# Preamble reordered on VectorE and ScalarE, the keys' norm table in one chain, and five unread products on TensorE between its first steps

## The chip, the cores and the metric

The kernel runs on one core of a Trainium2 chip. The metric is device time in microseconds (us) of one execution, lower is better. TensorE (PE, with its weight loads PEld), VectorE (DVE), ScalarE (ACT), GpSimd (POOL) and SyncE (SP) each take their own instructions in the order in which they were put down, and wait for each other through semaphores. Transfers are issued by SP, POOL and ACT.

## The reference

A decoder trunk of two layers over 512 tokens of width 2048. Each layer normalises its input, projects it once to 7696 columns, feeds three groups of heads, and projects the result back into the residual stream:

```python
def _layer(x, norm_g, w_in, conv_w, conv_b, sb_qn_g, sb_kn_g, gla_w_up, gla_b_up, gla_on_g, w_out):
    h = _rmsnorm(x, norm_g)                      # mean of squares over 2048, times a gain
    proj = h @ w_in                              # (512, 2048) @ (2048, 7696), split into 13 parts
    y_conv = _short_conv(cv_h, cv_b, cv_c, conv_w, conv_b) * silu(cv_g)
    q = _rmsnorm(sb_q.reshape(b, s, 8, 128), sb_qn_g)
    k = _rmsnorm(sb_k.reshape(b, s, 8, 128), sb_kn_g)
    y_sb = _stick_breaking(q, k, v) * silu(sb_g)
    g = log_sigmoid(gl_lr @ gla_w_up + gla_b_up) / 16
    y_gla = _rmsnorm(_gla(gl_q, gl_k, gl_v, g), gla_on_g) * silu(gl_g)
    return x + concatenate([y_conv, y_sb, y_gla]) @ w_out
```

## The kernel before

**Blocks and passes.** The 512 tokens are four blocks of 128 (`t` 0 to 3). The weights go through in blocks of 256 columns, listed in `specs`; the first of layer 0 are "gla v 0" (block 0), "gla v 1" with 16 narrow columns (block 1, 272 wide), "gla q" (block 2), "gla k" (block 3), "gla gate 0" (block 4). Every float32 operand is split into a float16 high half and a float16 low half, and each product is made of three: high by high, high by low, low by high. Weight blocks 0 and 1 are projected by token (`project_by_token`, line 857): 48 products for each token block, 16 of them high activations by high weights, 16 low activations by high weights, 16 high activations by low weights. Blocks 2 and 3 are projected by column (`project_cols`, lines 702 to 704) in two banks. Some later blocks, "gla gate 0" first, use fewer products on sums of token blocks (`xsums`, line 735; ACT's part is line 743).

**The preamble of layer 0.** For each token block: `xsquare(t)` sums squares on ACT, `xnorm` makes the scale (ACT and four small steps on DVE), `xgain(t, h)` multiplies half a block by scale and gain on DVE (h is the half of the 2048 columns), `xhigh(t, h)` transposes eight 128x128 pieces on TensorE (line 591) and copies them from PSUM as the float16 high half (line 593, tile `x`), and `xlow(t, h)` makes the low half: for block 0 on TensorE (line 603, adding the negative high half) and ACT (line 604), for the others by a subtraction on DVE (line 600). The gain row itself is spread over the partitions by twelve products (`spread`, line 244).

**The weights.** `fetch(i)` loads block i in two halves into one of two stage buffers (tile `st`). `wpeak0` and `wmax` square it on ACT (line 383), `wscale` turns the sums into a power of two (tile `ws`), `whi` or `whi0` writes the high half (tile `wh`, on ACT lines 445 and 454, on DVE line 447), `wlo` the low half (tile `wl`, line 461, DVE). For block 0 the sums over partitions are three small products (line 409). Blocks 0 to 2 are fetched by SP, later ones by POOL, each as soon as the last reader of its stage buffer is done.

**What sets the order.** On DVE and ACT the preamble is inside `tc.manual_schedule`: those calls stand in the written order. All else, and TensorE, SP and POOL throughout, is placed by a scheduler that follows priorities and dependencies; `order(a, b)` adds an edge without a wait. So the scheduler may put the token sums, the constants (`layer_consts`, lines 292 to 312) and the split of the results (`split_v`, lines 948 and 949) between preamble steps. Products by token and by column share one pool of three PSUM banks (`psp`), given out in turn: a bank is free when its readers are done, and for block 1 these are `split_v` and the copy of the 16 narrow columns (tile `lr`, line 975). The transposes use two double banks (`psz`).

**The norm table.** `layer_consts` transposes the small parameters (line 294) into `par` and for each layer on its own forms the product of the two norm gains, its maximum over partitions (POOL, line 183), a power of two (tiles `kpc`, `zun`), a diagonal matrix, and a product with ones (line 310), copied into `kg` (line 311).

Of the kernel before, what the change touches and what calls it, by code (L numbers as in the profile page):

```python
# [10 lines left out]
AF = mybir.ActivationFunctionType  # L11
# [6 lines left out]
P = 128  # L18
# [25 lines left out]
def hybrid_trunk(ctx, tc, x, norm_g, w_in, conv_w, conv_b, sb_qn_g, sb_kn_g,  # L44
# [193 lines left out]
    gps_ = [bank2(), bank2()]  # L238

    def spread(h):  # L240
        for a in range(2):
            r = 2 * h + a
            for i in range(3):
                T.matmul(gps_[h][:, a, :], identb[:4, r:r + 1].to_broadcast([4, P]), g3[:, i, :], start=i == 0,
                         stop=i == 2)
# [21 lines left out]
    for h in range(2):  # L267
        spread(h)
# [23 lines left out]
    def layer_consts():  # L292
        pps = bank(psm, "m")
        T.transpose(pps[:, :NP], prow, ident[:NP, :NP])
        V.tensor_copy(par, pps[:, :NP])
        for l in range(depth):
            V.tensor_reduce(onmax[:, l:l + 1], pcol("on", l), AX.X, ALU.max, apply_absolute_value=True)
            V.tensor_scalar(onmax[:, l:l + 1], onmax[:, l:l + 1], float(P) ** 0.5, None, ALU.mult)

            gq = sm(2, "cm")  # L300
            V.scalar_tensor_tensor(gq[:, 0:1], pcol("qn", l), float(P) ** -0.5, pcol("kn", l), ALU.mult, ALU.mult)
            V.tensor_scalar(gq[:, 1:2], allmax(gq[:, 0:1], 1, "k"), 2.0 ** -20, None, ALU.max)
            pow2(zun[:, l:l + 1], gq[:, 1:2], -20.0, "k")
            V.tensor_scalar(nzun[:, l:l + 1], zun[:, l:l + 1], -1.0, None, ALU.mult)
            V.reciprocal(gq[:, 1:2], zun[:, l:l + 1])

            dg = wk([P, P], "e")
            V.tensor_scalar(gq[:, 0:1], gq[:, 0:1], gq[:, 1:2], 2.0 ** -21, ALU.mult, ALU.mult)
            V.tensor_scalar(dg, ident, gq[:, 0:1], None, ALU.mult)
            T.matmul(pps[:, (l + 1) * P:(l + 2) * P], ones.to_broadcast([P, P]), dg, start=True, stop=True)  # L310
            V.tensor_copy(kg[:, l, :], pps[:, (l + 1) * P:(l + 2) * P])
            V.tensor_scalar(nbu[:, l, :], par[:, base["bu"] + 2 * l:base["bu"] + 2 * l + 2], -1.0, None, ALU.mult)
# [79 lines left out]
    def wscale(i):  # L392
# [10 lines left out]
        else:  # L403
# [4 lines left out]
            for j, (a, b) in enumerate(((ones, pk[:, 0:1]), (ones, pk[:, 1:2]), (pk[:, 2:3], pk[:, 2:3]))):  # L408
                T.matmul(ps, a.to_broadcast([P, P]), b, start=j == 0, stop=j == 2)
# [173 lines left out]
    xps = {}  # L583

    def xhigh(t, h, dst):
# [3 lines left out]
        for i in range(HK):  # L589
            k = h * HK + i  # L590
            T.matmul(ps[:, i, :], xv[:, k * P:(k + 1) * P], ident, start=i % 4 == 0, stop=True, is_transpose=True,
                     skip_group_check=True)
        S.activation(dst[0][:, t, h * HK:(h + 1) * HK, :], ps, AF.Copy)
# [49 lines left out]
    xsquare(1)  # L643
    wscale(0)
    whi0(0, 0, S)
    whi0(0, 1, V)
    xhigh(0, 1, mix)
# [6 lines left out]
    xlow(0, 1, mix, True)  # L654
    wlo(0, 0)
    wlo(0, 1)
    xhigh(1, 0, mix)
    xhigh(1, 1, mix)
    xsquare(2)
    xlow(1, 0, mix, False)  # L660
    xlow(1, 1, mix, False)
    xnorm(0, 2)
    xgain(2, 0)
    xgain(2, 1)
    xsquare(3)
    xnorm(0, 3)
    xhigh(2, 0, mix)
    xhigh(2, 1, mix)
    wmax(1, 0)
    xgain(3, 0)  # L670
    xgain(3, 1)
    xlow(2, 0, mix, False)
    xlow(2, 1, mix, False)
    wmax(1, 1)
    wscale(1)
    xhigh(3, 0, mix)
    xhigh(3, 1, mix)
    whi(1, 0)
    xlow(3, 0, mix, False)
    xlow(3, 1, mix, False)  # L680
    wlo(1, 0)
# [4 lines left out]
    for l in range(depth):  # L686
# [162 lines left out]
        def project_by_token(ah, al, n):  # L849
# [3 lines left out]
            for t in range(NT):  # L853
# [7 lines left out]
                ps.append(o)  # L861
                yield t, o, u
# [91 lines left out]
        if l == 0:  # L954
            layer_consts()
# [62 lines left out]
        for tag in ("qT", "kT"):  # L1018
# [520 lines left out]
```

## Time and profile before

| | before |
|---|---|
| median of 3 runs | 1634.72 us (1633.69 to 1635.13) |
| profiled execution | 1635.55 us |
| its span | 1633.8 us |
| PE, PEld busy | 1615.5 us (99%), 1356.8 us (83%) |
| DVE busy | 1446.2 us (89%) |
| ACT busy | 1196.5 us (73%) |
| POOL busy | 269.4 us (16%) |
| DMA moved | 235.98 MB, mean 144 GB/s |

The span runs from the first to the last instruction; the execution's time has some start and end around it. A matmul counts as busy from its start to the modelled end of its pipeline, so a busy TensorE may still be slow. The time from one start to the next tells its speed.

### The profile page before, as it was taken

How to read it: one execution, taken by the hardware profiler on the slowest of the kernel's cores; microseconds unless marked ns; L12 is line 12 of the kernel's file. 1: busy time of each engine (PE TensorE's matmuls, PEld its weight loads, DVE VectorE, ACT ScalarE, POOL GpSimd, SP SyncE). 2: the span in 40 equal slices, each digit the busy share in tenths (PEclk: the TensorE clock that was granted, in tenths of full speed). 3: DMA queues.
4: the chain of work that ended last, by engine and by line, in shares of the span. 5: the costliest groups of instructions: out<-in, count | busy, mean ns of one | idle time of the engine just before them, and what ended most of it. 6: DMA issues, size and time to landing. Idle time of an engine off the chain costs nothing.

```text
span 1633.8 us, 42252 instructions
## 1 busy us (share of the span) xinstructions
PE 1615.5 (99%) x18202; PEld 1356.8 (83%) x18202; DVE 1446.2 (89%) x2417; ACT 1196.5 (73%) x1771; POOL 269.4 (16%) x306
## 2 busy tenths in 40 slices
PE   8999999999999999999999999999999999999998
PEld 5757768989899968799996668689898989668998
DVE  7989989989898979898699899898998889898896
ACT  7668887977777776756775697788786868676573
POOL 0122021111212122011102111212121211220110
PEclk9999999999999999999999999999999999999999
DMA  7244435477767686644743544545777786773441
GB/s 262 81 103 145 89 119 111 106 164 144 169 150 169 150 169 186 177 148 147 244 94 107 127 117 103 144 89 137 155 158 160 153 165 150 161 229 130 156 157 54
DMA packets 193643, 235.98 MB, mean 144 GB/s; under 512 B 90242, under 2 KB 153036, under 8 KB 192944
## 3 DMA queue, kind: packets, MB, share of 16 engines
q0 software_dynamic: 79904, 181.42, 42.2%
q1 hardware_dynamic: 104544, 42.42, 13.4%
q10 hardware_dynamic: 9008, 9.45, 1.8%
q8 instruction: 142, 2.33, 0.6%
q14 instruction: 45, 0.37, 0.1%
HBM read 179.65 MB, written 14.68 MB: 119 GB/s over the span
## 4 chain that ended last, share of the span: by engine, by line
PE 68%; DVE 16%; ACT 7%; DMA 5%; issue 3%; POOL 1%; SPq 0%; DVEq 0%; ACTq 0%; POOLq 0%
PE psp L798 22%; PE psp L795 13%; PE psp L857 6%; PE psp L714 4%; PE psp L713 4%; PE psp L715 4%; PE psp L703 3%; PE psp L702 3%; DVE wl L509 3%; PE psp L704 3%; DMA st<-in_w_in_dram 3%; ACT wh L508 1%; PE psm L1345 1%; ACT junk L383 1%; PE psz L1305 1%
## 5 line engine op out<-in xcount | busy, mean ns | idle before, releaser
L508 ACT ACTIVATE wh<-st,ws 128x1024 f16<-128x1024 f32 x270 | 300.7, 1144 | 170.5 <-DVE st L528 89.8
L509 DVE SCALAR_TENSOR_TENSOR wl<-st,ws,wh 128x1024 f16<-128x1024 f32 x270 | 340.3, 1283 | 28.4 <-ACT wh L508 28.3
L383 ACT ACTIVATE junk<-st 128x2048 uint8<-128x2048 f32 x150 | 285.4, 1903 | 14.7 <-DMA st<-in_w_out_dram 6.9
L795 PE MATMUL psp<-s,wh 128*128 128x256 f16 x1280 | 217.7, 273 | 1.0 <-DVE g L811 0.9
L795 PEld LDWEIGHTS <-wh 128*128 128x128 f16 x1920 | 187.4, 98 | 23.3 <-issue 1.4
L798 PE MATMUL psp<-wh,s 128*128 128x128 f16 x2048 | 177.1, 219 | 0.5 <-issue 0.4
L795 PE MATMUL psp<-s,wl 128*128 128x256 f16 x640 | 174.3, 273 | 0.9 <-DVE wl L509 0.9
L713 PE MATMUL psp<-wh,m 128*128 128x256 f16 x640 | 174.5, 273 | 0.0
L715 PE MATMUL psp<-wh,m 128*128 128x256 f16 x640 | 174.5, 273 | 0.0
L714 PE MATMUL psp<-wl,m 128*128 128x256 f16 x640 | 174.5, 273 | 0.0
L798 PEld LDWEIGHTS <-s 128*128 128x128 f16 x3072 | 173.0, 98 | 0.8 <-issue 0.7
L798 PE MATMUL psp<-wl,s 128*128 128x128 f16 x1024 | 173.3, 219 | 0.0
L461 DVE SCALAR_TENSOR_TENSOR wl<-st,ws,wh 128x2048 f16<-128x2048 f32 x62 | 145.0, 2349 | 15.0 <-ACT wh L454 13.8
L362 POOL DMA_DIRECT2D st<-in_w_in_dram x114 | 109.7, 1030 | 246.4 <-DVE w7l L509 118.3
L798 PEld LDWEIGHTS <-m 128*128 128x128 f16 x2448 | 139.1, 98 | 2.1 <-issue 1.6
L454 ACT ACTIVATE wh<-st,ws 128x2048 f16<-128x2048 f32 x60 | 118.6, 1999 | 16.0 <-DVE ws L415 7.9
L399 POOL PARTITION_ALL_REDUCE wgm<-wm x75 | 48.1, 641 | 461.2 <-ACT junk L383 446.0
L386 POOL DMA_DIRECT2D st<-st x36 | 57.2, 1590 | 350.8 <-ACT junk L383 331.5
L795 PEld LDWEIGHTS <-wl 128*128 128x128 f16 x960 | 93.9, 98 | 14.4 <-issue 2.1
L798 PE MATMUL psp<-wh,m 128*128 128x128 f16 x1088 | 97.2, 219 | 0.4 <-DVE ws L415 0.4
L798 PE MATMUL psp<-wl,m 128*128 128x128 f16 x544 | 93.0, 219 | 0.0
L704 PEld LDWEIGHTS <-wl 128*128 128x128 f16 x384 | 37.6, 98 | 44.6
(448 smaller groups left out, 4193.5 us busy)
## 6 DMA issues: line engine op xcount, KB each, us to landing
st<-in_w_in_dram POOLq DMA_DIRECT2D x114, 1024.0 KB, 8.4
st<-in_w_out_dram POOLq DMA_DIRECT2D x32, 1024.0 KB, 8.3
st<-st POOLq DMA_DIRECT2D x36, 512.0 KB, 6.6
st<-in_w_in_dram SPq DMA_DIRECT2D x6, 1024.0 KB, 12.0
mixd<-g POOLq DMA_DIRECT2D x20, 256.0 KB, 7.6
x<-in_x_dram SPq DMA_DIRECT2D x4, 1024.0 KB, 5.2
qT<-in_x_dram ACTq DMA_DIRECT2D x8, 512.0 KB, 4.1
qT<-xs ACTq DMA_DIRECT2D x8, 512.0 KB, 12.2
```

Of the source, the lines that this page charges most:

```text
L362: load = queue.dma_start(s_, src[l, h * HK * P:(h + 1) * HK * P, c0:c0 + GW].rearrange("(k p) n -> p k n", p=P), max_dma_last_dim=1024)
L383: sq = S.activation(junk(HK * GW).rearrange("p (k n) -> p k n", k=part.shape[1]), part, AF.Square, accum_out=peak[i][:, h:h + 1])
L454: hi = S.activation(wh[:, :, :GW], staged[i][h], AF.Copy, scale=scales[i])
L461: a = V.scalar_tensor_tensor(wl[:, :, :GW], staged[i][h], scales[i], wh[:, :, :GW], ALU.mult, ALU.subtract)
L508: hi = S.activation(h_, b, AF.Copy, scale=sc)
L509: V.scalar_tensor_tensor(l_, b, sc, h_, ALU.mult, ALU.subtract)
L713: T.matmul(o, ah[:, t, k, :], wh[:, kk, :n], start=st_, stop=False, skip_group_check=True)
L714: T.matmul(o, ah[:, t, k, :], wl[:, kk, :n], start=False, stop=False, skip_group_check=True)
L715: return T.matmul(o, al[:, t, k, :], wh[:, kk, :n], start=False, stop=en, skip_group_check=True)
L795: mm = T.matmul(o, w[q_][:, kk, :], a[p_][:, :, kk, :], start=st_, stop=en, skip_group_check=True)
L798: mm = T.matmul(o[:, t * P:(t + 1) * P], a[p_][:, t, kk, :], w[q_][:, kk, :], start=st_, stop=en, skip_group_check=True)
L857: mm = T.matmul(o[:, :n], a_[:, t, k, :], w[k // HK][part][:, k % HK, :n], start=i == 0 and k == 0, stop=i == 2 and k == KT - 1)
```

## The change

- On TensorE three products of 512 columns, whose result nobody reads, follow `spread`, and two follow the small sums of block 0's peaks (`fill`). They write a bank of `psp` that is never read.
- `xhigh(0, 1)` stands ahead of `wscale(0)` and its copy goes from ACT to DVE; the first quarter of `whi0` goes from ACT to DVE.
- The rest of the written order changes: `xsquare`, `xnorm`, `xgain`, `xhigh`, `xlow` and `wlo` of the blocks are interleaved differently.
- The first half of the token sums of layer 0 gets an edge behind `wlo(1, 0)`; the first `split_v` gets one behind the high half of (2, 0).
- `layer_consts` stands behind the last transposes and treats both layers at once; its product moves into `key_gains`, behind the second token block of weight block 1.

```diff
+    idle = bank(psp, "p")
+    filled = []
+    def fill(n, behind):
+        for _ in range(n):
+            mm = T.matmul(idle.rearrange("p (a c) -> p a c", c=P), identb, identb[:, None, :].to_broadcast([P, 4, P]),
+                          start=True, stop=True)
+            order(mm, filled[-1] if filled else behind)
+            order(mm, behind)
+            filled.append(mm)
+        return mm
...
     for h in range(2):
-        spread(h)
+        mm = spread(h)
+    fill(3, mm)
...
     def layer_consts():
         pps = bank(psm, "m")
-        T.transpose(pps[:, :NP], prow, ident[:NP, :NP])
+        order(T.transpose(pps[:, :NP], prow, ident[:NP, :NP]), turned[3, 1])
...
-            V.tensor_scalar(gq[:, 1:2], allmax(gq[:, 0:1], 1, "k"), 2.0 ** -20, None, ALU.max)
-            pow2(zun[:, l:l + 1], gq[:, 1:2], -20.0, "k")
...
-            T.matmul(pps[:, (l + 1) * P:(l + 2) * P], ones.to_broadcast([P, P]), dg, start=True, stop=True)
-            V.tensor_copy(kg[:, l, :], pps[:, (l + 1) * P:(l + 2) * P])
...
+        gm = allmax(gq, depth, "k")
+        V.tensor_scalar(gm, gm, 2.0 ** -20, None, ALU.max)
+        pow2(zun, gm, -20.0, "k")
...
+    def key_gains(dg, behind):
+        ps = bank2()[:, 0, :depth * P]
+        order(T.matmul(ps, ones.to_broadcast([P, P]), dg.rearrange("p l c -> p (l c)"), start=True, stop=True), behind)
+        V.tensor_copy(kg, ps.rearrange("p (l c) -> p l c", c=P))
...
-                T.matmul(ps, a.to_broadcast([P, P]), b, start=j == 0, stop=j == 2)
+                mm = T.matmul(ps, a.to_broadcast([P, P]), b, start=j == 0, stop=j == 2)
+            fill(2, mm)
...
-        S.activation(dst[0][:, t, h * HK:(h + 1) * HK, :], ps, AF.Copy)
+        if eng is V:
+            V.tensor_copy(dst[0][:, t, h * HK:(h + 1) * HK, :], ps)
+        else:
+            marks[t, h] = S.activation(dst[0][:, t, h * HK:(h + 1) * HK, :], ps, AF.Copy)
...
     xsquare(1)
+    xhigh(0, 1, mix, V)
     wscale(0)
-    whi0(0, 0, S)
+    whi0(0, 0, V)
     whi0(0, 1, V)
-    xhigh(0, 1, mix)
     whi0(1, 0, V)
...
+            if not l and not t:
+                order(begun, marks[2, 0])
...
+            if not l and t == 1:
+                key_gains(dg, toktail[0])
...
+                if not l:
+                    for a in steps[:len(steps) // 2]:
+                        order(a, lows[1])
```

The rest of the written order is new as well. The parts on DVE and ACT behind xgain(1, 1), by call, were: xlow(0,0), xlow(0,1), wlo(0,0), wlo(0,1), xhigh(1,0), xhigh(1,1), xsquare(2), xlow(1,0), xlow(1,1), xnorm(2), xgain(2,0), xgain(2,1), xsquare(3), xnorm(3), xhigh(2,0), xhigh(2,1), and so on. They are now: xlow(0,0), xlow(0,1), xsquare(2), wlo(0,0), xnorm(2), xhigh(1,0), xhigh(1,1), xlow(1,0), xsquare(3), xgain(2,0), wlo(0,1), xlow(1,1), xnorm(3), xhigh(2,0), xgain(2,1), wmax(1,0), xlow(2,0), xgain(3,0), wmax(1,1), xhigh(2,1), wscale(1), and so on.

The built program shows it at three places. The instructions' lines are those of each kernel's own file: lines 591, 600, 603, 735, 857, 949, 975 of the kernel before are 614, 627, 630, 762, 884, 977, 1006 now. On TensorE, from block 0's transposes to the first product of weight block 0 (weight loads and repeated rows left out), before:

```order
L591 MATMUL psz_215<-ident,x_86 128x128 x8
L591 MATMUL psz_242<-ident,x_86 128x128 x8
L409 MATMUL psm_228<-wm_29_208,ones 128x1 x2
L409 MATMUL psm_228<-wm_29_208 128x1
L603 MATMUL psz_215<-x_185,ga_160 128x512
L857 MATMUL psp_413<-wh_238,x_185 128x256
```

And now, where psp_119 is the bank that is not read:

```order
L245 MATMUL psp_119<-identb 128x512
L614 MATMUL psz_219<-ident,x_86 128x128 x8
L614 MATMUL psz_231<-ident,x_86 128x128 x8
L430 MATMUL psm_242<-wm_30_212,ones 128x1 x2
L430 MATMUL psm_242<-wm_30_212 128x1
L245 MATMUL psp_119<-identb 128x512
L630 MATMUL psz_219<-x_189,ga_164 128x512
L630 MATMUL psz_231<-x_189,ga_164 128x512
L884 MATMUL psp_419<-wh_254,x_189 128x256
```

The two low-half products of the second half (psz_231) moved from behind the first eight products to ahead of them, and unread products stand at two places. On DVE, between the low halves of token blocks 2 and 3 (x_186 is the low half, psz the transposed block; zw, g are scratch of the token sums), before:

```order
L735 TENSOR_TENSOR zw_1135<-zw_1135,x_186 128x1024
L411 TENSOR_SCALAR wq_361<-wq_361 128x1
L189 TENSOR_SCALAR kpc_646<-cm_641 128x1
L735 TENSOR_TENSOR zw_1136<-x_185,zw_1135 128x1024
L415 TENSOR_SCALAR ws_367<-wq_361 128x1
L417 TENSOR_SCALAR wu_369<-wq_361,inoff_156 128x1
L600 TENSOR_TENSOR x_186<-psz_371,x_185 128x1024
L190 TENSOR_SCALAR kpc_646<-kpc_646 128x1
L600 TENSOR_TENSOR x_186<-psz_381,x_185 128x1024
```

And now (x_190 is the low half):

```order
L437 TENSOR_SCALAR ws_371<-wq_365 128x1
L439 TENSOR_SCALAR wu_373<-wq_365,inoff_160 128x1
L627 TENSOR_TENSOR x_190<-psz_355,x_189 128x1024
L603 SCALAR_TENSOR_TENSOR x_87<-x_87,xrs_333,g_210 128x1024
L1014 TENSOR_SCALAR gu_415<-wu_373 128x1
L627 TENSOR_TENSOR x_190<-psz_376,x_189 128x1024
L483 SCALAR_TENSOR_TENSOR wl_388<-st_177,ws_371,wh_387 128x8x256
L762 TENSOR_TENSOR g_1130<-x_189,x_190 128x1024
L486 SCALAR_TENSOR_TENSOR wl_388<-kT_180,ws_371,wh_387 128x8x16
L310 COPY par<-psm_623 128x42
L627 TENSOR_TENSOR x_190<-psz_392,x_189 128x1024
```

The sums moved from ahead of block 3's low halves to behind `wlo(1, 0)`, one of them ahead of the last low half. On DVE, the readers of the third token block's bank of weight block 1, before:

```order
L949 SCALAR_TENSOR_TENSOR v_408<-psp_821,v_408 128x256
L975 TENSOR_SCALAR lr_872<-psp_821,wu_369 128x16
L735 TENSOR_TENSOR zw_1154<-x_185,g_1156 128x1024
L978 CAST qT_677<-lr_872 128x48
```

And now:

```order
L977 SCALAR_TENSOR_TENSOR v_414<-psp_814,v_414 128x256
L762 TENSOR_TENSOR zw_1147<-x_189,g_1149 128x1024
L327 TENSOR_SCALAR e_645<-ident,cm_632 128x128 x2
L1011 TENSOR_TENSOR lr_806<-lr_806,qT_667 128x16
L1011 TENSOR_TENSOR lr_744<-lr_744,qT_667 128x16
L483 SCALAR_TENSOR_TENSOR wl_739<-st_416,ws_730,wh_738 128x8x256
L762 TENSOR_TENSOR zw_1147<-zw_1147,x_190 128x1024
L1009 CAST qT_667<-lr_806 128x48
L1009 CAST qT_667<-lr_744 128x32
L977 SCALAR_TENSOR_TENSOR v_414<-psp_873,v_414 128x256
L762 TENSOR_TENSOR zw_1148<-x_189,zw_1147 128x1024
L1006 TENSOR_SCALAR lr_865<-psp_814,wu_373 128x16
```

The second reader (L1006) moved away from the first (L977), behind one `wlo` and three sums; the bank's next user is the second bank of "gla q". TensorE now runs that block's first bank through both halves of the weights before it begins the second; before, it changed banks after the first half.

More of the change, by code (lines that the diff above doesn't have):

```diff
@@ L243, in spread @@
             for i in range(3):
-                T.matmul(gps_[h][:, a, :], identb[:4, r:r + 1].to_broadcast([4, P]), g3[:, i, :], start=i == 0,
-                         stop=i == 2)
+                mm = T.matmul(gps_[h][:, a, :], identb[:4, r:r + 1].to_broadcast([4, P]), g3[:, i, :], start=i == 0,
+                              stop=i == 2)
+        return mm
     def gain_copy(h):
@@ L298, in layer_consts @@
             V.tensor_scalar(onmax[:, l:l + 1], onmax[:, l:l + 1], float(P) ** 0.5, None, ALU.mult)
[L300 to L312 removed]
+            V.tensor_scalar(nbu[:, l, :], par[:, base["bu"] + 2 * l:base["bu"] + 2 * l + 2], -1.0, None, ALU.mult)
+        gq = sm(depth, "cm")
+        for l in range(depth):
+            V.scalar_tensor_tensor(gq[:, l:l + 1], pcol("qn", l), float(P) ** -0.5, pcol("kn", l), ALU.mult, ALU.mult)
+        gm = allmax(gq, depth, "k")
+        V.tensor_scalar(gm, gm, 2.0 ** -20, None, ALU.max)
+        pow2(zun, gm, -20.0, "k")
+        V.tensor_scalar(nzun, zun, -1.0, None, ALU.mult)
+        V.reciprocal(gm, zun)
+        V.scalar_tensor_tensor(gq, gq, 2.0 ** -21, gm, ALU.mult, ALU.mult)
+        dg = wk([P, depth, P], "e")
+        for l in range(depth):
+            V.tensor_scalar(dg[:, l, :], ident, gq[:, l:l + 1], None, ALU.mult)
+        return dg
+    def key_gains(dg, behind):
+        ps = bank2()[:, 0, :depth * P]
+        order(T.matmul(ps, ones.to_broadcast([P, P]), dg.rearrange("p l c -> p (l c)"), start=True, stop=True), behind)
+        V.tensor_copy(kg, ps.rearrange("p (l c) -> p l c", c=P))
     quick = set()
@@ L581, in xgain, with xhigh @@
         V.scalar_tensor_tensor(xv, xv, xscale[t], gb[h], ALU.mult, ALU.mult)
-    xps = {}
-    def xhigh(t, h, dst):
+    toktail = [None]
+    xps, marks, turned = {}, {}, {}
+    def xhigh(t, h, dst, eng=None):
         xv = xt[t // 2][:, t % 2, :]
@@ L590, in xhigh @@
             k = h * HK + i
-            T.matmul(ps[:, i, :], xv[:, k * P:(k + 1) * P], ident, start=i % 4 == 0, stop=True, is_transpose=True,
-                     skip_group_check=True)
-        S.activation(dst[0][:, t, h * HK:(h + 1) * HK, :], ps, AF.Copy)
+            mm = T.matmul(ps[:, i, :], xv[:, k * P:(k + 1) * P], ident, start=i % 4 == 0, stop=True, is_transpose=True,
+                          skip_group_check=True)
+        turned[t, h] = mm
+        if eng is V:
+            V.tensor_copy(dst[0][:, t, h * HK:(h + 1) * HK, :], ps)
+        else:
+            marks[t, h] = S.activation(dst[0][:, t, h * HK:(h + 1) * HK, :], ps, AF.Copy)
     def xlow(t, h, dst, on_pe):
@@ L654, in hybrid_trunk @@
     xlow(0, 1, mix, True)
+    xsquare(2)
     wlo(0, 0)
-    wlo(0, 1)
+    xnorm(0, 2)
     xhigh(1, 0, mix)
     xhigh(1, 1, mix)
-    xsquare(2)
     xlow(1, 0, mix, False)
+    xsquare(3)
+    xgain(2, 0)
+    wlo(0, 1)
     xlow(1, 1, mix, False)
[L662 to L665, printed above, removed]
     xnorm(0, 3)
     xhigh(2, 0, mix)
+    xgain(2, 1)
+    wmax(1, 0)
+    xlow(2, 0, mix, False)
+    xgain(3, 0)
+    wmax(1, 1)
     xhigh(2, 1, mix)
-    wmax(1, 0)
-    xgain(3, 0)
+    wscale(1)
+    xlow(2, 1, mix, False)
+    xhigh(3, 0, mix)
     xgain(3, 1)
[L672 to L677, printed above, removed]
     whi(1, 0)
     xlow(3, 0, mix, False)
+    xhigh(3, 1, mix)
+    wlo(1, 0)
     xlow(3, 1, mix, False)
-    wlo(1, 0)
     whi(1, 1)
@@ L861, in project_by_token @@
                 ps.append(o)
+                toktail[0] = mm
                 yield t, o, u
@@ L953, in hybrid_trunk @@
             begun = split_v(gv[0], t, o[:, :GW])
-        if l == 0:
-            layer_consts()
+            if not l and not t:
+                order(begun, marks[2, 0])
+        dg = layer_consts() if l == 0 else None
         V.tensor_scalar(gu[:, 0:1], u, 2.0 ** 35, None, ALU.mult)
```

## Prediction

> **What bounds the kernel now.** I read the page first (busy shares), then the stretches of the span, then what TensorE waited for, then the first 75 us instruction by instruction.
>
> ```profile
> PE 1615.5 (99%) x18202; PEld 1356.8 (83%) x18202; DVE 1446.2 (89%) x2417; ACT 1196.5 (73%) x1771; POOL 269.4 (16%) x306
> ```
>
> TensorE is the bound. Where its 18 idle microseconds lie is in the table of stretches; its columns are start and end, length, then busy time and count for PE, weight loads, DVE, ACT and POOL, granted clock, DMA share, GB/s.
>
> ```profile
> 18.00:36.00 18.00, 17.65 (x134) 14.53 (x134) 15.96 (x41) 12.95 (x21) 0.40 (x1) 1.00 0.83 248
> 36.00:54.00 18.00, 15.53 (x136) 13.18 (x135) 17.74 (x30) 16.22 (x19) 0.93 (x2) 1.00 0.06 18
> 54.00:74.00 20.00, 20.00 (x176) 16.95 (x175) 19.40 (x43) 10.08 (x14) 2.77 (x3) 1.00 0.34 110
> 74.00:300.00 226.00, 225.39 (x2048) 159.40 (x2046) 210.94 (x402) 178.01 (x265) 42.44 (x47) 1.00 0.46 115
> 300.00:1400.00 1100.00, 1096.01 (x12895) 944.81 (x12893) 975.88 (x1612) 823.20 (x1280) 194.20 (x215) 1.00 0.63 148
> ```
>
> After 74 us PE idles 0.6 us in 226 and 4.0 in 1100: time won before 74 us stays won if nothing else becomes the pace. Before that it idles 2.5 us in 36 to 54 us, where DVE is full (17.74 of 18). PE's waits there, in us, times, longest:
>
> ```profile
> PE psp L857 <- ACT wh L445: 1.3, 1, 1.3
> PE psz L591 <- DVE x L600: 1.2, 1, 1.2
> PE psp L857 <- ACT wh L456: 0.6, 1, 0.6
> PE psp L857 <- DVE kpc L190: 0.6, 1, 0.6
> PE psp L857 <- ACT x L593: 0.2, 1, 0.2
> ```
>
> Four of these (1.2, 0.6, 0.6, 0.2) lie after 30 us. The other loss is speed (rows: start, length, engine, line):
>
> ```profile
> 6.05 3.57 PE L244 MATMUL psz<-qp,identb 4*128 4x512 bf16 x8
> 11.22 3.68 PE L591 MATMUL psz<-ident,x 128*128 128x128 f32 x16 [1.60 <-DVE x L581]
> 15.40 0.57 PE L409 MATMUL psm<-wm 128*128 128x1 f32 x2
> 15.82 1.01 PE L603 MATMUL psz<-x,ga 128*128 128x512 f16 x2
> 18.11 1.87 PE L857 MATMUL psp<-wh,x 128*128 128x256 f16 x8 [1.27 <-ACT wh L445]
> 20.62 3.20 PE L857 MATMUL psp<-wh,x 128*128 128x256 f16 x16
> 24.54 1.04 PE L857 MATMUL psp<-wh,x 128*128 128x256 f16 x8
> 30.05 1.92 PE L857 MATMUL psp<-wh,x 128*128 128x256 f16 x16
> 31.81 1.91 PE L857 MATMUL psp<-wl,x 128*128 128x256 f16 x16
> 33.56 1.91 PE L591 MATMUL psz<-ident,x 128*128 128x128 f32 x16
> ```
>
> Sixteen products follow each other in 1.76 us at 30.05 (0.11 each), but eight take 1.87 at 18.11 and sixteen 3.20 at 20.62 (about 0.2 each): half speed until about 23.4, though the granted clock is written as 1.00 all along. The full speed comes 5.3 us after 18.11, the end of the last gap. A run's length holds a tail of about 0.16 beyond its last start, so a wait of 0.6 costs about 0.8.
>
> **The change, part by part.**
>
> *Three fills at the start.* By the row at 6.05 one costs 3.57 / 8 = 0.45, so 1.3 in all. They stand in the 1.60 that PE idles before 11.22: free, and followed by a gap again.
>
> *x(0,1) copied on DVE, whi0(0,0) on DVE, two fills.* Rows for these:
>
> ```profile
> 16.57 1.41 DVE L447 TENSOR_SCALAR wh<-st,ws 128x1024 f16<-128x1024 f32 x2
> 27.13 2.35 DVE L600 TENSOR_TENSOR x<-psz,x 128x1024 f16<-128x1024 f32 x2
> 22.60 4.61 DVE L461 SCALAR_TENSOR_TENSOR wl<-st,ws,wh 128x2048 f16<-128x2048 f32 x2
> 20.33 1.92 ACT L604 ACTIVATE x<-psz 128x1024 f16<-128x1024 f32 x2
> 27.40 1.90 ACT L630 ACTIVATE junk<-x 128x2048 uint8<-128x2048 f32 x1
> 29.86 1.89 ACT L630 ACTIVATE junk<-x 128x2048 uint8<-128x2048 f32 x1
> ```
>
> The DVE copy from PSUM is not in the trace; the nearest row is L600 (also PSUM, same size) at 1.17, and I take that. Half of it and twice it, 0.6 and 2.35, are its ends. From the transposes' end at 14.90 it runs to 16.07, so the scale chain starts 0.07 later, two quarters of 0.70 end at 18.1, the first after 17.35. On PE the two fills (0.9) run from 15.97 to 16.85 and the four L603 to 18.5. The first product stands at 18.45 instead of 18.11. At 2.35 for the copy it would be 19.3. But PE has then run from 15.8 without a gap, so with the same 5.3 us the full speed comes at 21.1, not 23.4.
>
> *To the third token block.* Of the 32 products of block 0, 12 run at 0.22 and 20 at 0.11: 23.3. The 16 transposes of block 1 end at 25.05. ACT's copies (0.96 each) end at 25.2 and 26.1, then xsquare(3) with its two small steps takes 2.46 (27.40 to 29.86), then ACT copies x(2,0), whose transposes PE ends at 29.6, so ACT runs 29.65 to 30.6. Block 2's first products start at 30.65: a new wait of 1.1, because this copy now stands directly before its user. Counting PE's rows, 64 products are then done in both kernels (before at 30.05), and three half blocks are transposed against two, 0.88 of work. So the lead is 0.88 - 0.60 = 0.3.
>
> *From there to the third weight block.* Rows:
>
> ```profile
> 38.86 1.09 PE L591 MATMUL psz<-ident,x 128*128 128x128 f32 x8 [1.19 <-DVE x L600]
> 43.06 1.22 DVE L735 TENSOR_TENSOR zw<-zw,x 128x1024 f32<-128x1024 f32 x1
> 44.31 1.22 DVE L735 TENSOR_TENSOR zw<-x,zw 128x1024 f32<-128x1024 f16 x1
> 46.76 0.15 DVE L190 TENSOR_SCALAR kpc<-kpc 128x1 int32<-128x1 int32 x1
> 45.90 0.39 PE L310 MATMUL psm<-e,ones 128*128 128x128 f32 x2
> 56.03 3.87 PE L857 MATMUL psp<-wh,x 128*128 128x272 f16 x32
> 68.99 0.28 PE L981 MATMUL psm<-identb,qT 128*128 128x128 bf16 x2
> 70.85 0.42 DVE L949 SCALAR_TENSOR_TENSOR v<-psp,v 128x256 f16<-128x256 f32 x1
> 73.97 0.38 PE L702 MATMUL psp<-x,wh 128*128 128x512 f16 x1
> 74.18 0.38 PE L703 MATMUL psp<-x,wh 128*128 128x512 f16 x1
> ```
>
> In the old order DVE runs token sums (L735) at 43.06 and 44.31 while the low halves of block 3 (L600) wait behind them; the wait called kpc is for such an L600, since kpc only ends beside it. In the new order the first sums stand behind wlo(1,0) and only one is ahead of the last low half, so these waits lose their cause. Going through the new rows with these durations, the tightest operands are: the copy x(2,1), at 36.85 behind two weight peaks of 2.0 on ACT, where PE asks at 36.8; the low half of (3,1), at 45.0 on DVE, asked for at 45.9; and the high half of the second weight block, at 48.5 on ACT, asked for at 49.4. PE's work from 30.65: 128 products at 0.11 (14.0), 192 of 272 columns at (3.87 - 0.16) / 32 = 0.116 (22.3), three half blocks of transposes (2.6), the constants' transpose (0.1), and 0.2 for such small waits: 69.85. The old row stands at 73.97, so 4.1 is won: 0.3 from before, four waits with tails 2.6 + 4 x 0.16 = 3.2, two kg products (L310, 0.22 each without the tail) moved out 0.4, and the rest rounding.
>
> *Norm table in one chain.* On DVE nine small rows go (0.07 to 0.2 each, 0.6 to 1.8). PE makes one product of 256 columns instead of two of 128, now inside the third block: twice 0.22. Two more of the small L981 also come later (0.28 for two with the tail, some 0.06 each). So 0.5 goes back. Left: 4.1 - 0.5 = 3.6.
>
> *The banks.* The third block's second bank is freed by L975's successor, now 11 rows behind its split_v instead of directly behind it. From the low half of (3,1) at 45.0 to it stand on DVE 15 sums (1.14 each: 43.06 to 44.31 less two small rows), three wlo (4.61 / 2 = 2.3), six split_v (0.34 to 0.42) and some 40 small rows of 0.07 to 0.2: 29 to 35 us, so 74 to 80. PE asks at 69.85 + 48 x 0.21 + 0.4 = 80.3, because it now runs the first bank through both halves first. Free, with nothing to spare at the worst end.
>
> [...] The row at 20.62 shows half speed to its end, 5.3 us after the last gap. [...]
>
> **Rivals.**
>
> (A) The full speed is not earlier, still 23.4. The gap before 18.11 speaks against it; that PE ran from 11.22 to 16.8 without speeding up speaks for it. Then 22 of block 0's products are slow, 1.1 us: gain 2.5, 1632.2. [...]
>
> (B) DVE paces layer 0. In 18 to 74 us it idled 2.04 + 0.26 + 0.60 = 2.9; it takes on 1.17 + 0.70 and loses 0.6 to 1.8, so its own work ends 1.0 to 2.8 earlier, not 3.6. For it: 210.94 busy of 226 behind. Against: 15 us idle there, and PE waited 0.6 in all. Taking 2.1 of gain, in the upper half: 1632.6.
>
> (C) Slower, by the third block's load. SP issues it when wlo(0,1) has read the stage buffer, and wlo(0,1) moves from the end of the run of two wlo to behind the norm of block 2 (0.9), xlow(1,0) (1.17) and xgain(2,0) (2.48 / 2): with the first wlo ending at 24.2, 0.7 earlier than before, DVE ends it at 24.2 + 3.3 + 2.3 = 29.8, against 27.2.
>
> ```profile
> 31.00 2.48 DVE L581 SCALAR_TENSOR_TENSOR x<-x,xrs,g 128x1024 f32<-128x1024 f32 x2
> 29.20 1.01 SPq L362 DMA_DIRECT2D st<-in_w_in_dram  x2
> 30.00:38.00 8.00, 7.43 (x65) 6.24 (x65) 7.82 (x30) 6.26 (x9) 0.40 (x1) 1.00 0.85 262
> ```
>
> Before, it was issued at 29.20 and moved until 38 at the latest (share 0.85 of 8 us). In the new ACT order its peak (wmax(2,0)) stands before the copy x(3,1), with which PE goes on; ACT comes to it at 39.7. Each microsecond of landing past about 40.3 is a microsecond of PE. It eats the gain at 43.9 and makes the kernel 0.2% slower from 47 on: 1638. The issue is only some 0.6 later, which speaks against it.
>
> (D) The waits only change place: gain 0 to 1.5 through the bank above or the copies x(2,1) and x(3,0), which stand behind two weight peaks of 2 us on ACT. 1634.
>
> **Numbers.** The profiled execution took 1635.55 (span 1633.8 and 1.75 around it), 0.8 above the median 1634.72 of the three runs. 1635.55 - 3.6 = 1631.95, and against the median 1631.1. Chances: forecast 0.60, A 0.12, B 0.15, C 0.07, D 0.06. Half the total chance lies beyond 3.3 us, that is 0.2%, about what a measurement of this kernel can tell from no change: of the forecast's 0.60 I give 0.50 to gains above it and 0.10 to 2.9 to 3.3. So faster 0.50; same 0.43 (0.10 + A + B + D); slower 0.07. The low end takes full speed at the first product already (block 0 done at 21.9, then ACT holds block 2 until 29.5, 1.2 more), none of the 0.2 of small waits, and 0.7, half the spread of the three runs: gain 5.7, 1629.0. The high end is D at 1634.3; outside are C and the tails.
>
> **What the new profile would show.** Right: five rows of fills, none delaying a product much past 18.5; products at 0.11 spacing from about 21; one wait of about 1 us for the copy x(2,0) near 30; no wait for L600's successor or kpc after that; the third block's first product near 69.9 and a kg product inside it; waits after 74 us no more than 1 us above the old ones. Wrong: waits for DVE at the third block's second bank, for ACT at blocks 2 and 3, or products at 0.2 spacing past 23.

## The result, and the profile after

The changed kernel took 1628.33 us (median of 6 executions, 1627.87 to 1629.31) against 1634.20 of the kernel before in the same comparison: ratio 0.9967, 95% interval 0.9957 to 0.9977. Two later comparisons, in the experiments below, gave 0.9968 (0.9957 to 0.9980) and 0.9964 (0.9950 to 0.9977). Over all executions seen here the medians are 1628.46 (19 executions) and 1633.54 (113, from 1631.70 to 1636.50): 5.1 us, 0.31%. The forecast was 1631.1 with a gain of 3.6 and a low end of 1629.0. The sign was right, the size was not, and the time lies 0.7 under the range. The gain of this comparison, 5.9, is more than the 5.7 of the low end; that over all executions, 5.1, is less.

The timeline of TensorE in the changed kernel, from the fills to the third weight block; columns are start, length, engine, line, tiles, shapes, count, and in brackets the idle time before with what ended it:

```profile
9.50 1.46 PE L245 MATMUL psp<-identb 128*128 128x512 bf16 x3
11.24 3.68 PE L614 MATMUL psz<-ident,x 128*128 128x128 f32 x16 [0.28 <-DVE x L603]
15.60 0.59 PE L245 MATMUL psp<-identb 128*128 128x512 bf16 x2
16.03 1.02 PE L630 MATMUL psz<-x,ga 128*128 128x512 f16 x4
17.46 4.11 PE L884 MATMUL psp<-wh,x 128*128 128x256 f16 x32 [0.41 <-DVE wh L469]
27.43 1.06 PE L614 MATMUL psz<-ident,x 128*128 128x128 f32 x8
29.62 1.05 PE L884 MATMUL psp<-wh,x 128*128 128x256 f16 x8 [1.12 <-ACT x L620]
...
69.17 0.38 PE L729 MATMUL psp<-x,wh 128*128 128x512 f16 x1
73.48 0.59 PE L332 MATMUL psz<-e,ones 128*128 128x256 f32 x2
```

The two later fills take 0.22 us each, and so do the four products of L630: full speed, from about 15.3 us on in the trace's record of the granted clock. The 32 products of block 0 take 4.11, and not the 5.0 that the forecast's 12 slow and 20 fast ones make with their tail. The third weight block's first product stands at 69.17 against 73.97 before, 4.8 earlier. What TensorE waited for in the whole execution, the six largest:

```profile
PE psz L257 <- ACT qp L234: 3.0, 1, 3.0
PE psp L884 <- ACT x L620: 1.6, 2, 1.1
PE psp L822 <- DVE wq L433: 0.5, 1, 0.5
PE psp L822 <- DVE wl L531: 0.4, 1, 0.4
PE psp L822 <- DVE g L838: 0.4, 1, 0.4
PE psp L884 <- DVE wh L469: 0.4, 1, 0.4
```

The waits for a low half of x (1.2 before), for kpc (0.6), for ScalarE's high halves of the first two weight blocks (1.3 and 0.6) are gone; the one for ScalarE's copy x(2,0) is new. Windows of the changed kernel, each with length, busy time of TensorE, weight load, VectorE, ScalarE and GpSimd, granted clock, DMA share and GB/s:

```profile
18.00:36.00 18.00, 16.25 (x141) 13.89 (x139) 17.62 (x33) 15.87 (x23) 1.00 (x1) 1.00 0.80 242
36.00:54.00 18.00, 17.98 (x161) 15.54 (x160) 17.97 (x33) 12.71 (x16) 3.42 (x4) 1.00 0.17 49
54.00:74.00 20.00, 20.00 (x156) 15.24 (x154) 20.00 (x38) 13.58 (x15) 2.24 (x3) 1.00 0.29 93
```

From 36 to 74 us both TensorE and VectorE are busy without a break.

### The profile page after: what moved, and what is told of

It is laid out like the page before. It is cut to its first block, busy times and chain, and to the rows that moved or that the text cites. A ratio compares the mean times of both kernels' runs of the same rounds, so it can differ in the third digit from the quotient of the medians.

```text
span 1626.7 us, 42256 instructions
## 1 busy us (share of the span) xinstructions
PE 1614.1 (99%) x18205; PEld 1355.0 (83%) x18205; DVE 1446.8 (89%) x2411; ACT 1196.5 (74%) x1769; POOL 274.0 (17%) x305
## 4 chain that ended last, share of the span: by engine, by line
PE 79%; DVE 11%; ACT 6%; issue 2%; DMA 1%; POOL 0%; SPq 0%; DVEq 0%; ACTq 0%; POOLq 0%
PE psp L825 25%; PE psp L822 15%; PE psp L884 6%; PE psp L742 6%; PE psp L741 6%; PE psp L740 6%; PE psp L730 4%; PE psp L729 4%; PE psp L731 3%; DVE wl L531 2%; PE psm L1379 2%; PE psz L1339 1%; ACT wh L530 1%; ACT junk L404 1%; DMA x<-in_x_dram 1%
## 5 line engine op out<-in xcount | busy, mean ns | idle before, releaser
L404 ACT ACTIVATE junk<-st 128x2048 uint8<-128x2048 f32 x150 | 285.4, 1903 | 14.2 <-DMA st<-in_w_in_dram 7.3
L420 POOL PARTITION_ALL_REDUCE wgm<-wm x75 | 52.8, 704 | 454.4 <-ACT junk L404 426.5
```

Of the source, the lines that this page charges most:

```text
L404: sq = S.activation(junk(HK * GW).rearrange("p (k n) -> p k n", k=part.shape[1]), part, AF.Square, accum_out=peak[i][:, h:h + 1])
```

## The experiments

Two questions come first: which part of the change brings the gain, and whether it is the clock (then the fills would do) or the waits (then the order would). The change has four parts, called here **fills** (five unread products), **order** (the written order of the start on VectorE and ScalarE), **sums** (the edges that hold the first layer's token sums back behind the first low part of the second weight block) and **norms** (the keys' norm table in one chain, with one product of 256 columns inside the third block). In what follows "block 2" is the first product of the third token block, and "third block" the start of the third weight block's first product, both in the profiled execution. Times are medians.

**The kernel before and the changed kernel, a second profile of each.** No edit.

> The kernel before, once more, for its profile alone. Two questions. The clock: by the theory that TensorE's own run of work sets it, products are at full spacing from 22 to 25 us again, since the gap before 18.1 us is the same; by the rival that the point falls at random, anywhere from 19 to 25. The waits after 400 us (0.5 and 0.4 us at 406 to 412, 0.9 at 638, 0.35 at 1156, 0.45 at 1289 in the first profile, all but half of one absent in the changed kernel's): by the theory that these differ from execution to execution, at least two of them are missing or elsewhere here; by the rival that the old preamble causes them, all stand at the same places within 0.2 us.

> The changed kernel, once more, for its profile. The clock: full spacing from 15 to 16 us again if the fills set it, anywhere from 13 to 23 if the point falls at random. The third block's first product at 69.2 within 0.3 us by the first theory, up to 70.2 by the second. After 400 us: waits of 0.3 us and more reappear if they differ between executions (span 1626.7 to 1628), none if the new preamble removed them (span 1626.7 within 0.3).

Measured: 1634.06 and 1627.97; third block 74.78 and 69.02. The clock of the kernel before turned at 14.07 us this time instead of 23.25, and still nothing was won; that of the changed kernel turned at 13.03, ahead of the 15 to 16 that the first theory of the fills gave. Rows of the kernel before's timeline, two windows, and its starts of block 2 and of the third block:

```profile
18.71 1.87 PE L857 MATMUL psp<-wh,x 128*128 128x256 f16 x8 [2.88 <-ACT wh L445]
21.22 3.42 PE L857 MATMUL psp<-wh,x 128*128 128x256 f16 x16
...
16.00:18.00 2.00, 0.00 (x0) 0.00 (x0) 1.22 (x4) 2.00 (x3) 0.00 (x0) 0.87 1.06 442
18.00:20.00 2.00, 1.29 (x7) 0.89 (x7) 0.00 (x0) 1.97 (x5) 0.00 (x0) 0.50 0.98 364
...
30.87 1.92 PE L857 MATMUL psp<-wh,x 128*128 128x256 f16 x16
74.78 0.38 PE L702 MATMUL psp<-x,wh 128*128 128x512 f16 x1
```

TensorE waited 2.88 us for ScalarE's cast of the first weight, which stands behind a square of 1.91 there. In that pause the clock fell back to half (0.50) until 24.3, so that 16 products took 3.42 us. The waits that the first profile of before had at 406, 412, 638 and 1289 us, 2.3 us together, are not in this one. From block 2 to the third block it is 43.91 us in both profiles of the kernel before (30.05 to 73.97, 30.87 to 74.78), and 39.55 in both of the changed kernel: that stretch is the same whenever the clock turned, and what differs between two profiles of a kernel lies ahead of it or behind.

**Fills: the changed kernel without them, and the kernel before with them alone.**

```diff
-    fill(3, mm)        # behind the constants' products
-            fill(2, mm)    # behind the first weight's column sums
```

> The changed kernel without the five unread products, all else the same. If the fills turn the clock early: full spacing only from 20 to 23 us, block 2's first products 0.5 to 1 us later, the third block's first product at 69.8 to 70.3, 0.6 to 1.2 us slower than the changed kernel, so 4.2 to 5.2 us faster than before. If the early clock was luck of one execution: the same time as the changed kernel within 0.4 us (5.4 to 5.9 us faster than before).

> The kernel before with the five unread products and nothing else. If they turn the clock early: full spacing from 15 to 20 us, block 0's 32 products done 1.5 to 2.5 us sooner, of which block 1 keeps 0.5 to 1.5, since ACT's copies and the two wlo on DVE then hold it: 0.3 to 1.5 us faster. If the point falls at random: within 0.4 us of before, with half spacing past 20 us.

Measured: without fills 1629.25 (ratio to before 0.9978, 0.9969 to 0.9987), third block 68.72; fills alone 1633.16 (1.0000, 0.9990 to 1.0009), third block 72.92. Without fills the third block came earlier than with them (the clock turned at 14.18, which the first theory did not expect), and yet the time was longer: what was lost lies behind the third block. By the medians the fills are worth 0.7 to 0.9 in the changed kernel, by the ratios 1.6 to 2.3 with intervals that overlap, and nothing that can be measured alone: there the cast of the first weight holds TensorE up as before, although the clock turned at 13.55:

```profile
17.98 1.03 PE L878 MATMUL psp<-wh,x 128*128 128x256 f16 x8 [2.28 <-ACT wh L461]
```

**Order, sums and norms, each taken out of the changed kernel, and the order alone.**

```diff
 # old order: back to the sequence of before, among it
-    xhigh(0, 1, mix, V)
+    xhigh(0, 1, mix)
-    whi0(0, 0, V)
+    whi0(0, 0, S)
 # old sums: without
-                    for a in steps[:len(steps) // 2]:
-                        order(a, lows[1])
-                order(begun, marks[2, 0])
 # old norms: layer_consts as before, without
-                key_gains(dg, toktail[0])
```

> The changed kernel with the written order of the first layer's start put back as it was (copy of x(0,1) on ScalarE, second half of the first weight block cast by ScalarE, squares and norms at their old places); fills, held-back token sums and the one-chain norm table stay. Theory 1 (the written order carries the gain): the first product comes at about 18 us behind ScalarE's cast again and waits of about 1.3 at block 2 and 1.2 at the last low half come back; the third weight block's first product at 72 to 73 us instead of 69.0; time 1631.5 to 1632.5. Theory 2 (the norm table and the held-back sums carry it, by freeing VectorE between 36 and 54 us): third block near 70, time below 1630.

> The changed kernel without the two edges that hold the first layer's token sums back, all else as changed. Theory 1 (only the written order counts; the scheduler places the sums in gaps anyway): third block's first product within 0.3 us of 69.0, time 1628.0 to 1628.6. Theory 2 (the sums then stand ahead of a low half or of a weight's low part on VectorE, as rows L735 did at 43.06 and 44.31 before): TensorE waits 1 to 2.4 us in 40 to 54 us, third block at 70 to 71.4, time 1629.2 to 1630.5.

> The changed kernel with the keys' norm table built as before, in its two steps on VectorE with two products of 128 columns. Theory 1 (the table is worth its wait of 0.6 us called kpc and its two products of 0.22, less 0.3 that the one product costs inside the third block): time 0.5 to 0.9 longer, 1628.6 to 1629.1. Theory 2 (the wait called kpc was one for the low half and is gone with the order): no more than 0.2 us either way, 1628.0 to 1628.3. Theory 3 (VectorE, without an idle moment from 36 to 74 us, sets the pace there, so that its nine small rows count in full): 0.6 to 1.8 longer, 1628.7 to 1630.0.

> The kernel before with the new written order alone: no fills, sums not held back, norm table as before. Theory 1 (the order carries nearly all): third block's first product at 69.5 to 70.5 us, time 1629 to 1630. Theory 2 (the order needs the held-back sums, which otherwise stand ahead of low halves on VectorE): third block at 71 to 72.5, time 1630.5 to 1632.

| kernel | block 2 to third block | third block | time | ratio to before (95%) |
|---|---|---|---|---|
| all but the order | 42.03 | 70.08 | 1638.40 | 1.0027 (1.0016 to 1.0039) |
| all but the sums | 40.64 | 70.55 | 1629.48 | 0.9977 (0.9969 to 0.9986) |
| all but the norms | 39.85 | 70.31 | 1637.43 | 1.0026 (1.0017 to 1.0035) |
| the order alone | 40.73 | 71.13 | 1631.50 | 0.9988 (0.9979 to 0.9997) |

The first column says where the gain of the changed kernel between 30 and 74 us comes from. It falls from 43.91 to 39.55, of which 0.88 is a half block of transposes that the new order does ahead of block 2. Of the other 3.5 the order alone brings 2.3, the sums on top of it 0.9 to 1.1 and the norms 0.1 to 0.3 (fills and order without the two, further down, have 40.73). The sums and the order alone came out as their second theories had it.

Two of the times no theory expected: without the order, or without the norms, the kernel is slower than before, although its third block starts 3.7 to 3.9 earlier than in the first profile of before. The loss lies behind it, most of it near 120 us; the profile without the norms, the slowest of its eleven executions (1640.91), has further waits of 1.42 and 1.57 us at 194 and 561. Timeline of TensorE without the norms, then one row without the order, then a window of each:

```profile
123.28 0.28 PE L816 MATMUL psp<-s,wl 128*128 128x256 f16 x1 [2.71 <-DVE wl L525]
124.91 0.42 PE L816 MATMUL psp<-s,wl 128*128 128x256 f16 x1
...
125.21 0.40 PE L822 MATMUL psp<-s,wl 128*128 128x256 f16 x1 [4.30 <-DVE wl L531]
...
124.00:128.00 4.00, 4.00 (x23) 2.96 (x22) 3.36 (x11) 1.58 (x2) 1.81 (x2) 0.57 0.27 52
124.00:128.00 4.00, 2.79 (x14) 1.99 (x15) 4.00 (x10) 2.15 (x2) 0.43 (x2) 0.61 0.00 0
```

Both wait for a weight's low part on VectorE (2.71 and 4.30), and both then lose more: the clock falls to half for 3.41 us (0.57 and 0.61 over the window), at 124.26, 1.0 behind the end of the first pause, and at 124.92, inside the second; half of that, up to 1.7 us, is lost. VectorE of the changed kernel and of the one without norms, around the last cast of the low-rank gate (L1009 and L1002), with ScalarE's first row of the gate at the end of each:

```profile
84.26 0.18 DVE L1009 CAST qT<-lr 128x32 bf16<-128x32 f32 x1
84.41 1.23 DVE L762 TENSOR_TENSOR s<-zw,s 128x1024 f16<-128x1024 f32 x1
86.31 4.61 DVE L483 SCALAR_TENSOR_TENSOR wl<-st,ws,wh 128x2048 f16<-128x2048 f32 x2
96.57 0.69 ACT L1023 ACTIVATE ga<-psm,par 128x512 f32<-128x512 f32 x1 [4.48 <-PE psm L1020]
```

```profile
84.11 2.33 DVE L477 SCALAR_TENSOR_TENSOR wl<-st,ws,wh 128x2048 f16<-128x2048 f32 x1
86.54 1.21 DVE L756 TENSOR_TENSOR s<-zw,s 128x1024 f16<-128x1024 f32 x1
88.47 2.33 DVE L477 SCALAR_TENSOR_TENSOR wl<-st,ws,wh 128x2048 f16<-128x2048 f32 x1
91.94 0.17 DVE L1002 CAST qT<-lr 128x32 bf16<-128x32 f32 x1
101.38 0.69 ACT L1016 ACTIVATE ga<-psm,par 128x512 f32<-128x512 f32 x1 [5.08 <-PE psm L1013]
```

In the changed kernel the casts end at 84.4, before the last sum and the two low parts of the fourth weight block. Without the norms the scheduler, whose times have shifted, puts both low parts and the sum first; the casts end at 92.1 and the gate begins 4.8 later. What hangs on the gate (scans, exponentials, casts) then meets the next weight's work on ScalarE and VectorE, and its low part is late. That was a reading until the next runs.

**One edge that puts the gate's casts first**, in the two slow kernels:

```diff
+                    lrlast[0] = V.tensor_copy(lr3[:, t, b:b + n, :], ...)
...
+                    order(lows[3], lrlast[0])
```

> The changed kernel with the old norm table, as in the run that took 1637.4, and one edge more: the low part of the fourth weight block on VectorE stands behind the last cast of the low-rank gate (L1009 in the changed kernel), as it does in the changed kernel's own order. Theory 1 (the late gate chain is what costs: those casts stood behind a sum and two low parts, so the gate's product came at 100.8 instead of 95.8 us and everything VectorE had to do before 120 us came in one heap): no wait of more than 0.6 us near 120 us, time 1629 to 1630. Theory 2 (the nine small rows and the two products of the old table cost it by themselves): 1635 or more.

> The changed kernel with the old written order, as in the run that took 1638.4, and the same one edge. Theory 1 (late gate chain): no wait of more than 0.6 us near 120 us, time 1629.5 to 1631, which is the price of the order alone, some 1 to 2 us. Theory 2 (the written order itself is worth 9 us): 1636 or more.

Measured: without norms 1630.62 instead of 1637.43 (ratio to before 0.9982, 0.9974 to 0.9991), and no wait of the kind near 120; this one edge is worth 6.8 us, so the late gate is the cause that theory 1 named for the norms. The time lies 0.6 above that theory's range; the norms' own price is then about 2. Without the order 1634.72 instead of 1638.40 (1.0006, 0.9997 to 1.0015): 3.7 of the 9.9 that it is slower than the changed kernel. There the gate's first half came earlier, its second still late (its product on TensorE at 106.39, in the changed kernel's second profile at 100.97), and three waits remain behind 118 us:

```profile
106.39 0.38 PE L1021 MATMUL psm<-e,kT 128*128 128x512 bf16 x1
119.06 0.28 PE L822 MATMUL psp<-s,wh 128*128 128x256 f16 x1 [0.79 <-ACT wh L530]
120.10 0.28 PE L822 MATMUL psp<-s,wh 128*128 128x256 f16 x1 [0.76 <-ACT wh L530]
122.15 0.28 PE L822 MATMUL psp<-s,wl 128*128 128x256 f16 x1 [1.77 <-DVE wl L531]
```

So for the old order the late gate is shown as part of the cause only, and theory 1's 1631 was missed by 3.7.

**Two parts without the others.** The kernel before with fills and order, and with fills and sums (edits as above). In both the scheduler puts the gate's casts early by itself.

> The changed kernel without the held-back sums and with the old norm table, so fills and written order only. Its order on the engines has the gate's casts early. Theory 1 (parts add up where the gate chain is early): 1630 to 1630.8, third block's first product near 70.9 us, no wait near 120 us. Theory 2 (old norms cost 8 us in any company): 1635 or more.

> The kernel before with the fills and the held-back sums alone: old written order, old norm table; the gate's casts stand early. Theory 1 (parts add up): the held-back sums win 1.1 to 1.5 us at the third block, whose first product comes near 71.6 us, no wait near 120 us, time 1631.3 to 1632.3. Theory 2 (holding the sums back always overfills VectorE before 120 us): a wait of 2.5 us or more there and 1635 or more.

Measured: fills and order 1630.76 (0.9984, 0.9975 to 0.9993), third block 71.22; fills and sums 1629.86 (0.9978, 0.9969 to 0.9987), third block 71.33. The second is better than either theory said. VectorE with fills alone, then with fills and sums:

```profile
39.12 1.22 DVE L756 TENSOR_TENSOR g<-x,x 128x1024 f32<-128x1024 f16 x1
44.59 1.21 DVE L621 TENSOR_TENSOR x<-psz,x 128x1024 f16<-128x1024 f32 x1
...
41.81 1.21 DVE L621 TENSOR_TENSOR x<-psz,x 128x1024 f16<-128x1024 f32 x1
46.76 1.22 DVE L756 TENSOR_TENSOR g<-x,x 128x1024 f32<-128x1024 f16 x1
```

The first sum stood at 39.12 ahead of the low half at 44.59; held back, it comes at 46.76 and the low half at 41.81. The third block gains 1.6. The medians differ by 3.3, though, and the rest isn't explained: the executions with fills alone spread from 1631.8 to 1636.0, those with fills and sums from 1629.6 to 1631.3.

**What was still open: the size, the clock's price, and which wait ends last.** The changed kernel again; with the transposes of x(2,0) eight products earlier on TensorE; without the first three fills; another profile without all five.

```diff
 # earlier transposes
+                        if cursor[0] == 1 and not l and t == 1 and i == 1 and k == 0:
+                            order(mm, turned[2, 0])
 # no first fills
-    fill(3, mm)
```

> The changed kernel as it is, on the same chip and in the same rounds as the next two. Theory 1 (the change is worth what the starts of the third block say, 5.0 to 5.6 us, and the waits near 406, 412, 638 and 1289 us in the first profile of before were chance): 1627.9 to 1628.5, 5.0 to 5.6 below before. Theory 2 (those later waits belong to the kernel before, and the change takes them away too): 7 us below before.

> The changed kernel with the eight transposes of x(2,0) on TensorE eight products earlier, nothing else moved on any engine. Theory 1 (the wait of 1.1 us for ScalarE's copy x(2,0) is on the path): the transposes start at 26.4 instead of 27.3, the wait shrinks to 0.3, and the third block's first product comes 0.5 to 0.9 us earlier, 1627.1 to 1627.6. Theory 2 (VectorE, busy without a break from 36 to 74 us, sets the end of layer 0's first blocks): the wait comes back at a low half or a weight's low part before 50 us, third block at 69.0, time as the changed kernel within 0.2.

> The changed kernel without the first three unread products (those before the transposes of x(0,*)); the later two stay. Theory 1 (the first three count, by closing the gap of 1.4 us before 11 us, so that in executions where the clock would turn only after 20 us it turns before 16): 0.8 to 1.3 above the changed kernel, like the run without all five. Theory 2 (the later two count, by keeping TensorE from pausing before the first products): within 0.3 of the changed kernel.

> Another look at the changed kernel without its five unread products. Where its clock turns before 15 us, the third block's first product comes at 68.7 as in the first look and the time is 1628.7 to 1629.0; where it turns after 20 us, at 70 to 70.6 and 1629.6 to 1630.4.

| kernel | clock turned at | third block | time | ratio to before (95%) |
|---|---|---|---|---|
| changed | 19.08 | 69.40 | 1628.57 | 0.9968 (0.9957 to 0.9980) |
| earlier transposes | 13.48 | 68.39 | 1628.09 | 0.9969 (0.9956 to 0.9981) |
| no first fills | 19.63 | 69.72 | 1629.42 | 0.9978 (0.9970 to 0.9987) |
| no fills, one execution | 20.15 | 69.46 | 1630.51 | |

The gain is 4.8 here, nearer to theory 1 than to the 7 of theory 2. The first three fills are the ones that count, 0.85 by the medians. A late turn of the clock costs 0.3 to 0.7 at the third block (69.40 to 69.72, against 68.72 to 69.17 where it turned by 15.4), less than the 70 to 70.6 expected of the last row. Since it comes late in half of the profiles without the first fills, and in two of fourteen with them, that is 0.1 to 0.3 of the 0.85 on average, an estimate. The rest arises behind the third block: from there to the end of the span it is 1557.1 to 1557.5 us in the four profiles of the changed kernel, and 1558.7 to 1559.2 in the three without the first fills, which have waits of 0.3 to 0.8 near 403, 409, 634, 662 or 1152. With the order alone, also without fills, it is 1557.3, so why these waits come is open. Rows of a late turn, changed kernel and one execution without fills:

```profile
18.04 4.17 PE L884 MATMUL psp<-wh,x 128*128 128x256 f16 x32
...
17.12 5.14 PE L869 MATMUL psp<-wh,x 128*128 128x256 f16 x32
```

The transposes did what they should: the wait of 1.12 for the copy x(2,0) is 0.24 and the lead of 0.5 to 1.0 on the four profiles of the changed kernel lasts to the third block. From block 2 to the third block it is 39.55 in all nine profiles of the changed kernel, with or without fills and with earlier transposes: there TensorE's own work sets the time, and that wait ended last ahead of it. The time, 1628.09, is 0.5 above theory 1's range.

```profile
26.66 1.07 PE L614 MATMUL psz<-ident,x 128*128 128x128 f32 x8
28.84 1.05 PE L884 MATMUL psp<-wh,x 128*128 128x256 f16 x8 [0.24 <-ACT x L620]
...
68.39 0.38 PE L729 MATMUL psp<-x,wh 128*128 128x512 f16 x1
```

**Does that lead reach the end?** The same two kernels once more.

> The changed kernel with the eight transposes of x(2,0) eight products earlier, a second time, beside the changed kernel. Theory 1 (the 0.6 to 1.0 us that the third block's first product gained in the first profile lasts to the end): median 0.5 to 1.0 below the changed kernel's. Theory 2 (it is taken back by waits after 300 us that come and go between executions): medians within 0.3 of each other.

> The changed kernel as it is, for the comparison with the run above: 1628.3 to 1628.7, 4.8 to 5.4 below before.

Measured: 1627.74 (ratio to before 0.9963, 0.9950 to 0.9975) and 1628.21 (0.9964, 0.9950 to 0.9977). The medians are 0.5 apart, as in the pair above, but the intervals overlap almost wholly, and in these two profiles the third block is only 0.1 apart (68.77 and 68.88). The wait for the copy is 0.24 again, but TensorE now stands still before the eight transposes:

```profile
27.03 1.06 PE L614 MATMUL psz<-ident,x 128*128 128x128 f32 x8 [0.56 <-issue]
...
25.66 1.27 DVE L603 SCALAR_TENSOR_TENSOR x<-x,xrs,g 128x1024 f32<-128x1024 f32 x1
```

The view names no engine for it; VectorE's `xgain(2, 0)` (L603), whose result they transpose, ends at 26.93. So with the transposes moved, VectorE is what ends last there. The version beats the kernel before; that it beats the changed kernel is likely and not shown.

## Why the prediction was right or wrong

*The sign, and where the gain comes from:* right. The four waits in layer 0 went, the first product did not come earlier by much, the new wait for the copy x(2,0) is 1.12 (forecast 1.1) and from there TensorE runs nearly through.

*The step that failed: full speed at 21.1 us, 5.3 after a gap at 15.8.* The prediction let each pause start the count anew. The fills left no such gap: TensorE has no idle time above 0.41 from 9.5 to 21, and the clock turned at 15.3. In the fourteen profiles with all five fills, of whatever kernel, it turned between 12.4 and 15.4 in twelve and at 19.1 in two; in the six without the first three, at 13.8 to 14.2 in three and at 19.6 to 23.3 in three: so the fills make an early turn more frequent, as far as so few can show, and chance has a part in it. The first product came at 17.46 instead of 18.45, block 2 at 29.62 instead of 30.65, the third block at 69.17 instead of 69.85. So the lead at block 2, which the forecast put at 0.88 - 0.60 = 0.3, was 0.88 + 0.44 = 1.3, and what was won from there 3.5 instead of 3.8. A late turn takes back only a little of it: with one at 19.1 the third block still starts at 69.40.

*The term of 4.1 at the third block* was mis-sized by this step and by its reference row. The mean of the four profiles of the changed kernel is 69.12: 4.9 earlier than the first profile of before, 5.7 earlier than the second, about 5.3. The old row of 73.97 was one draw; the other is 74.78. Of what is missing, 0.7 is the new start and 0.4 the old row. Of the four profiles in which TensorE pauses 1.85 to 2.88 us before its first products, three lost the clock again (behind 1.85, 2.63 and 2.88; not behind 2.28), and the new order took that pause away as well (at most 0.64 in the changed kernel): a gain that no part of the sum had.

*The 0.5 given back for the products inside the third block:* right in kind, 0.4 in size (VectorE's rows at 360 us lie 5.2 earlier than in the second profile of before, the third block 5.6).

*The reference.* The sum went against 1634.72, three executions; over 113 the kernel before takes 1633.54. Of the 2.7 by which 1631.1 misses the overall 1628.46, 1.2 is this and 1.5 is the gain of 5.1 that was put at 3.6. The low end had all of the clock's best case in it, but not a reference lower by 1.2: from 1633.54 its gain of 5.7 would have led to 1627.8. That the time fell under the range is thus in part the luck of three executions, the wrong step is not.

*The bank of the third block and the waits behind 74 us:* right for the changed kernel; the reader L1006 of that bank ran at 74.25, at the early end of the 74 to 80 given, and no wait stands there.

*Rivals.* (A), (B) and (C) did not decide it. The clock turned before 23.4, and between 36 and 74 us TensorE has no wait in which (C) could show. VectorE is busy throughout from 36 to 74 us, but so is TensorE, whose 39.55 from block 2 on do not change from profile to profile; ahead of block 2, VectorE ends last once the transposes are moved. (By its own rows, (B)'s 1.0 to 2.8 is 1.6 to 2.8: 2.9 - 1.87 + 0.6 and + 1.8.) (D) did not come in the changed kernel, but waits that change place are what happens as soon as the order or the norms are left out, at 1638.4 and 1637.4 instead of the 1634 it was given. The prediction checked the bank behind the third block, and not where the gate's casts stand among the low parts; in the kernel without the norms that position decides between 4 us lost and 3 won.

*The turns of the clock.* In the second profile of before the granted clock was full from 14.07, half from 17.48 and full again from 24.31: 3.41 us at full speed, then 6.83 at half. Ahead of its turn at 14.07 TensorE did nothing but transposes from 10.95 on, so there the turn came during them; the 16 took 3.47 us, against 3.68 in the first profile, where the turn came at 23.25. In one profile (the old order with the edge) half speed came with a pause of 1.85 us, from 17.69 to 21.10:

```profile
17.84 1.87 PE L884 MATMUL psp<-wh,x 128*128 128x256 f16 x8 [1.85 <-ACT wh L467]
```

*Left open:* waits of 0.3 to 1.0 us near 385, 402 to 412, 638 and 1150 us that appear in some executions of nearly every kernel here and not in others, and with them the last microsecond of several medians.

## What to carry to other kernels

Where a scheduler places the rest of the program by its own times, parts of a change do not add: look, in the new order itself, for the long rows that have moved in front of a short chain with many dependents, far behind the edit. Here the kernel without one of two helpful parts is 4 to 5 us slower than before, and one edge gave 6.8 back in one case and 3.7 in the other. Before taking a difference of a few tenths of a per cent from one profile, take a second one of the old kernel.

## What was not expected of the hardware

TensorE lost its full speed again around five pauses of 1.85 to 4.30 us. Half speed lasted 3.41 us with those of 1.85, 2.63, 2.71 and 4.30, which cost up to 1.7 us on top of the pause, and 6.83 with that of 2.88, some 2.8 us; both costs are estimates, half of the half-speed time in which TensorE was not waiting. A pause of 2.28 us, with the fills alone, did not bring it (granted clock 1.00 from 0 to 54 us), one of 2.63, with fills and sums, did (0.81, 0.50 and 0.83 in the three windows of 2 us from 18 on):

```profile
17.94 1.03 PE L878 MATMUL psp<-wh,x 128*128 128x256 f16 x8 [2.63 <-ACT wh L461]
```

Nor did the waits of 0.79, 0.76 and 1.77 us near 120 us without the order, with the edge (1.00 from 74 to 300 us). So the length of a pause alone does not tell the two kinds apart: half speed came with 1.85 us in one profile and not with 2.28 in another. What decides it was not shown.
